# Gathered expert rows in four parts of 32 tokens: products of one table beside sums of the other

## The chip, the cores and the metric

The kernel runs on one core of one Trainium2 chip. The metric is the device time of one execution in microseconds. Three runs of the kernel before gave 3989.97, 3996.61 and 4001.97 us; the median is 3996.61.

## The reference, cut to what matters

Two layers, each a token mixer and then a product-key expert mixer ("peer"), over 512 tokens of width 1024. Only the expert mixer is touched. Each token picks 128 experts (8 heads, 16 each) out of 16384, and needs one row of table `u` and one of table `v` for each:

```python
def peer(h, w_q, sub_keys, u_emb, v_emb):
    q = (t @ w_q).reshape(n_tok, PEER_HEADS, 2, PEER_KEY_DIM // 2)
    scores = jnp.einsum('thpk,hpnk->thpn', q, sub_keys)
    ...
    best, pos = lax.top_k(cand, PEER_TOPK)
    expert = jnp.take_along_axis(cand_idx, pos, axis=-1)
    gates = jax.nn.softmax(best, axis=-1)
    ...
        u = u_emb[eb]
        act = jax.nn.gelu(jnp.einsum('td,thkd->thk', tb, u)) * gb
        return jnp.einsum('thk,thkd->td', act, v_emb[eb])
```

## The kernel before

The 512 tokens are four tiles of 128. Tiles 2 and 3 (`DT`) go the dense way: every row of both tables is read once, and a token's gate is zero for experts that it didn't pick. Tiles 0 and 1 (`GT`) go the gathered way: an indirect DMA fetches one table row for each of 128 partitions, so that 256 gathers a tile (128 of `u`, 128 of `v`) bring all it needs. Both ways run at the same time in one loop over 128 blocks of 128 experts.

The dense way, for block `b` (function `block`): `up` multiplies a block of `u` (24 bf16 matmuls `pu` of 256 columns: each fp32 operand is split in a high and a low bf16 half) and applies the gelu to give `H[b]`; DVE multiplies `H[b]` by the gate slice `G[:, j]` (tile `a`), ACT and DVE split it (`ah`, `al`), and twelve matmuls `acc` add `a` times the block of `v`. The weights come through `Stream.emit`: a 512 KB DMA, ACT makes `whi`, and GpSimd or, for 5 of 16 tiles, DVE makes `wlo`.

The gates are made in phases (`PHASES`): `gate_tile` holds the gates of 26 blocks (24 in the first phase) while those of the next phase are being made, in 16 groups of 16 tokens (`gate_group`). A group is an equality compare over all 128 keys (`o2`, 128x2048 elements), one over the phase's keys (`o1`), a multiply by the split gate, 16 small matmuls `pg`, two ACT copies `gs` and two adds into `G`. In the first phase the adds are GpSimd's; in all others everything but the copies is DVE's. The 16 groups of a phase are spread over the blocks of the phase before it; in the first phase they begin at block `LATE` = 13, when the routing of tile 1 is done, and must be done two blocks before the phase ends.

The gathered way (function `gathered`): a list `order` holds the gathers, first the 128 of `u` of tile 0, where partition t holds the row of token t, then the 128 of `v`, then the same for tile 1. A gather is queued on GpSimd (`gather`) right behind the newest weight split there, six places (`LEAD`) before its row is used; the rows lie in a ring of `ROWS` = 9 tiles. A `u` row is used by DVE: one `tensor_tensor_reduce` over 128x1024 (`products`, tile `junk`) gives 128 activations. Four `v` rows are used by PE (`sums`): eight fp32 matmuls, 32 columns of weights by 512, from which PE makes sixteen (`av`). The pace is set by `tick`, called once for each `up` and once for each block: it takes as many places of `order` as keep the list even over 222 ticks, a little over two each. Places taken before the loop (`EARLY_STEPS`) go beside the routing of tiles 2 and 3 and beside the first phase's 16 gate groups.

The order on each engine's queue is then set by a scheduler from the program's order and from explicit "issue after" constraints: products stand behind the newest split of `a`.

## Time and profile before

| | |
|---|---|
| Median of three runs | 3996.61 us |
| The profiled execution's own time | 3984.77 us |
| Its span, first to last instruction | 3982.9 us |
| PE, DVE, ACT, GpSimd busy | 79%, 73%, 37%, 66% of the span |
| Granted TensorE clock, mean | 0.883 |
| DMA | 923.70 MB, mean 232 GB/s |

The two layers stand one behind the other and read alike: in the first the expert mixer's early routing begins near 400 us, its gather queue at 501.8 us, its first gate phase at 640 us, and the loop over blocks runs from 729 to 1955 us; in the second the loop runs from 2739 to 3966 us. "Idle before" in a group's row is what its engine sat idle ahead of these instructions, and behind the arrows stands what ended it. DVE instructions overlap a little at their ends, so that the groups of a full stretch add up to some 6% more than the stretch.

### The profile page before, as it was taken

The numbers are of one execution on the slowest core, as the hardware profiler recorded it, in microseconds if no ns is written. First come the engines' busy times: TensorE is split into PE (matmuls) and PEld (weight loads), VectorE is DVE, ScalarE is ACT, GpSimd is POOL, SyncE is SP. The second block draws the span as 40 slices with busy tenths as digits, with TensorE's granted clock in tenths as the row PEclk, the third lists the DMA queues.
The fourth block names the chain that finished last, engine by engine and source line by source line (L and its number), as shares of the span: only waits on it lengthen the run. The fifth ranks groups of instructions, "written<-read, shape, count | busy, mean of one in ns | idle before, by whom it ended". The sixth has DMA issues, their size and how long they took to land. (4 is left out here: it accounts for less than half of the span.)

```text
span 3982.9 us, 53857 instructions
## 1 busy us (share of the span) xinstructions
PE 3138.0 (79%) x19594; PEld 1834.8 (46%) x19594; DVE 2911.0 (73%) x5135; ACT 1454.6 (37%) x2411; POOL 2638.5 (66%) x1721
## 2 busy tenths in 40 slices
PE   8999863567899766899898878635668997767998
PEld 4444552234455444454455545522344554444543
DVE  5553699998765999631568765999997559998524
ACT  5554432232333323332455564312323333333323
POOL 3446665665888878777433355657657888787875
PEclk9999986677999878999999999865778998888999
DMA  4324564576999888899621135654767999888997
GB/s 135 92 76 141 174 207 152 183 238 201 321 355 368 307 285 292 321 332 341 196 75 59 60 101 156 201 178 157 253 198 284 339 370 325 286 283 295 341 340 257
DMA packets 262346, 923.70 MB, mean 232 GB/s; under 512 B 29888, under 2 KB 39616, under 8 KB 262080
## 3 DMA queue, kind: packets, MB, share of 16 engines
q0 software_dynamic: 147456, 536.94, 37.8%
q1 hardware_dynamic: 104832, 372.84, 28.8%
q10 hardware_dynamic: 9792, 10.49, 0.9%
q8 instruction: 153, 2.51, 0.3%
q14 instruction: 113, 0.93, 0.1%
HBM read 918.05 MB, written 2.10 MB: 231 GB/s over the span
## 5 line engine op out<-in xcount | busy, mean ns | idle before, releaser
L81 POOL TENSOR_TENSOR wlo<-w,whi 128x1024 bf16<-128x1024 f32 x551 | 1220.9, 2220 | 596.9 <-ACT whi L80 554.3
L80 ACT ACTIVATE whi<-w 128x1024 bf16<-128x1024 f32 x696 | 731.5, 1053 | 829.3 <-DMA w<-ut_in 263.8
L764 POOL DMA_INDIRECT g<-u_in,ix x512 | 690.3, 1348 | 409.5 <-DVE hk L776 194.2
L776 DVE CUSTOM_DVE_ANT_0 junk<-g,hn 128x1024 bf16<-128x1024 f32 x512 | 754.7, 1474 | 6.1 <-DMA g<-u_in,ix 5.7
L764 POOL DMA_INDIRECT g<-v_in,ix x512 | 554.5, 1083 | 186.7 <-issue 94.3
L89 PE MATMUL pu<-hh,wlo 128*128 128x256 bf16 x2048 | 596.1, 291 | 72.6 <-DVE wlo L81 46.9
L87 PE MATMUL pu<-hh,whi 128*128 128x256 bf16 x2048 | 598.5, 292 | 29.5 <-ACT H L864 21.8
L88 PE MATMUL pu<-hl,whi 128*128 128x256 bf16 x2048 | 595.5, 291 | 0.0
L883 PE MATMUL pg<-o,o 128*128 128x52 bf16 (+1 forms) x2560 | 310.3, 282 | 355.0 <-DVE o L874 291.1
L81 DVE TENSOR_TENSOR al<-a,ah 128x256 bf16<-128x256 f32 x256 | 185.1, 723 | 510.9 <-ACT ah L80 507.5
L883 PEld LDWEIGHTS <-o 128*128 128x128 bf16 x2560 | 269.3, 149 | 431.0 <-DVE o L874 268.5
L88 PE MATMUL acc<-wlo,ah 128*128 128x512 bf16 x1024 | 433.3, 423 | 30.7 <-DVE wlo L81 29.4
L87 PE MATMUL acc<-whi,ah 128*128 128x512 bf16 x1024 | 376.0, 415 | 95.1 <-ACT ah L80 94.9
L89 PE MATMUL acc<-whi,al 128*128 128x512 bf16 x1024 | 422.8, 421 | 22.2 <-DVE al L81 22.0
L89 PEld LDWEIGHTS <-wlo 128*128 128x128 bf16 x2816 | 289.6, 103 | 202.4 <-DVE wlo L81 51.1
L799 PE MATMUL av<-g,z 128*32 128x512 f32 x2048 | 355.3, 605 | 17.5 <-DVE z L793 10.7
L87 PEld LDWEIGHTS <-whi 128*128 128x128 bf16 x2816 | 291.6, 104 | 153.9 <-issue 31.8
L88 PEld LDWEIGHTS <-whi 128*128 128x128 bf16 x2816 | 291.4, 103 | 138.6 <-issue 40.6
L885 ACT ACTIVATE gs<-pg 128x416 f32<-128x416 f32 (+1 forms) x320 | 163.3, 510 | 437.2 <-PE pg L883 427.1
L887 DVE TENSOR_TENSOR G<-gs 128x208 f32<-128x208 f32 x256 | 219.5, 860 | 86.2 <-ACT gs L885 85.9
L80 ACT ACTIVATE ah<-a 128x256 bf16<-128x256 f32 x256 | 105.8, 414 | 432.0 <-PE acc L88 196.1
L870 DVE TENSOR_TENSOR o<-iot,i2T 128x2048 bf16<-128x2048 bf16 x160 | 250.9, 1568 | 11.6 <-PE pg L883 11.2
(382 smaller groups left out, 5025.3 us busy)
## 6 DMA issues: line engine op xcount, KB each, us to landing
w<-ut_in SPq DMA_DIRECT2D x256, 512.0 KB, 5.3
w<-v_in SPq DMA_DIRECT2D x256, 512.0 KB, 5.0
w<-w_in SPq DMA_DIRECT2D x88, 512.0 KB, 3.6
w<-wo_in SPq DMA_DIRECT2D x64, 512.0 KB, 3.7
w<-wq_in SPq DMA_DIRECT2D x32, 512.0 KB, 3.6
key<-keys_in ACTq DMA_DIRECT2D x64, 128.0 KB, 3.2
g<-u_in,ix POOLq DMA_INDIRECT x512, 6.0
g<-v_in,ix POOLq DMA_INDIRECT x512, 7.0
```

What stands on the lines that cost most here:

```text
L80: nc.scalar.activation(hi, src, AF.Copy)
L81: return (lo_eng or nc.vector).tensor_tensor(lo, src, hi, op=OP.subtract)
L87: nc.tensor.matmul(out, ah, bh, start=start and i == 0, stop=False)
L88: nc.tensor.matmul(out, ah, bl, start=False, stop=False)
L89: nc.tensor.matmul(out, al, bh, start=False, stop=stop and i == n - 1)
L764: nc.gpsimd.indirect_dma_start(out=g, out_offset=None, in_=tab, in_offset=bass.IndirectOffsetOnAxis(ap=ix, axis=0))
L776: nc.vector.tensor_tensor_reduce(k.junk, g, hn[i], op0=OP.mult, op1=OP.add, scale=1.0, scalar=0.0, accum_out=h[:, s:s + 1])
L799: nc.tensor.matmul(av[c][32 * j:32 * j + 32, :], z[:, j, o:o + 32], rows[j][:, c * 512:(c + 1) * 512], start=r == 0, stop=r == 31)
L870: nc.vector.tensor_tensor(o2, iot, i2T[:, None, ts].to_broadcast([128, KEYS, GB]), op=OP.is_equal)
L883: nc.tensor.matmul(pv[:, t, :, :n], o2[:, :, c * 8 + t], o1[:, 1:3, :, c * 8 + t], start=True, stop=True)
L885: nc.scalar.activation(gs, pv[:, :, :, :n], AF.Copy)
L887: eng.tensor_tensor(G[:, :n, t0 + c * 8:t0 + c * 8 + 8], gv[:, 0], gv[:, 1], op=OP.add)
```

## The change

Three things change together.

1. The gathered tokens of a tile are taken in four parts (`PARTS`) of 32. In a gather of `u` the 128 partitions now hold 32 tokens times 4 experts each, so that 32 gathers serve a part; the part's own 32 rows of the normed input are copied four times over by matmuls with columns of the identity (`hr`). The list `order` now takes, in turns, four `u` gathers of part n and four `v` gathers of part n-1. The indices and gates of a tile are laid out for this at the end of its routing, by 32 small matmuls.
2. The eight `av` matmuls of four `v` rows are ordered behind the first of them, which waits for the row that comes last. The sums' two PSUM banks are held from the beginning, and `pg` in the first phase has 2 of them where it had 3.
3. `PHASES` is 18 and five times 22, six phases where there were five; `AHEAD` (the blocks whose `H` is made ahead) is 10 where it was 12, and the ring `ROWS` is 11 where it was 9. The compares at the end of the routing go in six pieces where they went in three.

```diff
-PHASES = [24, 26, 26, 26, 26]
+PHASES = [18, 22, 22, 22, 22, 22]
-AHEAD = 12
+AHEAD = 10
-ROWS = 9
+ROWS = 11
+PARTS = 4
...
+        def part(r):
+            return k.ident.rearrange("p (u r) -> p r u", r=PARTS)[:, r]
...
-            for j0, h0, nh in ((0, 0, 8), (8, 0, 4), (8, 4, 4)):
+            for j0, h0, nh in ((0, 0, 4), (0, 4, 4), (8, 0, 2), (8, 2, 2), (8, 4, 2), (8, 6, 2)):
...
-            def products(i, h):
-                for s in range(NS):
+            def products(i, r, h):
+                hr = work.tile([128, D], F32, tag="hr", name="hr", bufs=1)
+                for c in range(2):
+                    p = pr.tile([128, 512], F32, tag="r", name="phr")
+                    for q in range(4):
+                        nc.tensor.matmul(p[32 * q:32 * q + 32, :], part(r), hn[i][:, c * 512:(c + 1) * 512],
+                                         start=True, stop=True)
+                    nc.scalar.activation(hr[:, c * 512:(c + 1) * 512], p, AF.Copy)
+                for s in range(32):
                     g = yield
                     with after():
-                        nc.vector.tensor_tensor_reduce(k.junk, g, hn[i], op0=OP.mult, op1=OP.add, scale=1.0,
+                        nc.vector.tensor_tensor_reduce(k.junk, g, hr, op0=OP.mult, op1=OP.add, scale=1.0,
                                                        scalar=0.0, accum_out=h[:, s:s + 1])
-            def sums(i, h):
+            def sums(i, r, h, av):
...
+                    first = None
                     for c in range(2):
-                        for j in range(4):
-                            nc.tensor.matmul(av[c][32 * j:32 * j + 32, :], z[:, j, o:o + 32],
-                                             rows[j][:, c * 512:(c + 1) * 512], start=r == 0, stop=r == 31)
+                        for j in reversed(range(4)):
+                            with tc.issue_after(first.ins) if first is not None else nullcontext():
+                                m = nc.tensor.matmul(av[c][32 * j:32 * j + 32, :], z[:, j, a * 32:a * 32 + 32],
+                                                     rows[j][:, c * 512:(c + 1) * 512],
+                                                     start=r == 0 and a == 0, stop=r == PARTS - 1 and a == 7)
+                            first = first or m
...
-                for i in GT:
-                    order += [(ut, i, 0, s) for s in range(NS)]
-                    order += [(vt, i, 1, 32 * j + r) for r in range(32) for j in range(4)]
+                for n in range(len(parts) + 1):
+                    for a in range(8):
+                        if n < len(parts):
+                            order += [(n, 0, 4 * a + s) for s in range(4)]
+                        if n:
+                            order += [(n - 1, 1, 4 * a + j) for j in range(4)]
...
-                        pv = ahead.tile([128, 512], F32, tag="g", name="pg", bufs=3)
+                        pv = ahead.tile([128, 512], F32, tag="g", name="pg", bufs=2)
```

How the queues read. First GpSimd in the middle of layer 0's loop, where the gathers (`g`) and the weight splits (`wlo`) alternate. Before, in tile 0's sums:

```order
L764 DMA g<-v_in,ix_4182 128x1024 x4
L81 TENSOR_TENSOR wlo<-w_10389,whi 128x1024
L764 DMA g<-v_in,ix_4182 128x1024 x2
L81 TENSOR_TENSOR wlo<-w_10432,whi 128x1024
L764 DMA g<-v_in,ix_4182 128x1024 x2
L81 TENSOR_TENSOR wlo<-w_10492,whi 128x1024
```

After, at about the same place:

```order
L776 DMA g<-u_in,ix_4197 128x1024 x4
L82 TENSOR_TENSOR wlo<-w_9571,whi 128x1024
L776 DMA g<-v_in,ix_4197 128x1024 x2
L82 TENSOR_TENSOR wlo<-w_9622,whi 128x1024
L776 DMA g<-v_in,ix_4197 128x1024 x2
L776 DMA g<-u_in,ix_4197 128x1024 x2
```

The number of gathers between two splits is about the same; one table in long stretches has become both in turns of four.

Second, DVE in layer 0 at block 14 (`a` and `al` belong to a block, `o` and `G` to a gate group of the next phase, `junk` and `hk` to a product). Before, from block 14's `a` to block 15's:

```order
L922 TENSOR_TENSOR a_7135<-H,G 128x256
L870 TENSOR_TENSOR o_7165<-iot,i2T 128x2048
L81 TENSOR_TENSOR al<-a_7135,ah 128x256
L776 ISA junk,hk_4339<-g,hn_2721 128x1024
L776 ISA hk_4339 128x1
L872 TENSOR_TENSOR o_7167<-iot,i1T 128x416
...
L922 TENSOR_TENSOR a_7262<-H,G 128x256
```

After, from block 14's `a` to block 15's:

```order
L948 TENSOR_TENSOR a_7540<-H,G 128x256
L82 TENSOR_TENSOR al<-a_7326,ah 128x256
L915 TENSOR_TENSOR G<-gs 128x22x8
L795 ISA junk,hk<-g,hr 128x1024
...
L902 TENSOR_TENSOR o_7474<-o_7474,ghl 128x704
L82 TENSOR_TENSOR al<-a_7540,ah 128x256
...
L948 TENSOR_TENSOR a_7775<-H,G 128x256
```

Before, 18 rows stand between the two, with 2 gate groups and 4 products. After, 67 rows stand there, with 12 of the phase's 16 groups and 4 products, and 54 of them lie between block 14's `a` and its own `al`.

Third, PE in the sums of tile 1 (`av`) beside a block's matmuls (`acc`). Before, in layer 0:

```order
L89 MATMUL pu<-hh,wlo 128x256
L799 MATMUL av<-g,z 32x512 x2
L88 LDWEIGHTS ah
L88 MATMUL acc_6057<-wlo,ah 128x512
...
L799 MATMUL av<-g,z 32x512 x4
L87 LDWEIGHTS ah
L87 MATMUL acc_6057<-whi,ah 128x512
L799 MATMUL av<-g,z 32x512 x2
```

After, in the steady part of layer 0:

```order
L818 MATMUL av<-g,z 32x512 x4
L89 LDWEIGHTS ah
L89 MATMUL acc_6196<-wlo,ah 128x512
...
L818 MATMUL av<-g,z 32x512 x4
L88 LDWEIGHTS ah
L88 MATMUL acc_6196<-whi,ah 128x512
```

Before, the eight of a set were broken into runs of one to nine in tile 1's sums; after, they stand in runs of eight, or of four and four, in both tiles.

## Rows read from the trace of the kernel before

**Rows 1.** The page's 40 slices: DVE's busy share in tenths
```profile
DVE  5553699998765999631568765999997559998524
```
**Rows 2.** Windows of layer 0: us, busy us (instructions) per engine, granted clock, DMA share, GB/s
```profile
640.00:729.00 89.00, 31.48 (x266) 26.85 (x267) 89.00 (x121) 17.90 (x39) 67.37 (x52) 0.50 0.39 122
729.00:838.00 109.00, 60.69 (x222) 24.95 (x222) 108.36 (x303) 26.57 (x38) 64.83 (x43) 0.74 0.67 221
838.00:914.00 76.00, 51.97 (x324) 34.78 (x322) 73.08 (x96) 22.09 (x35) 47.75 (x31) 0.76 0.73 239
914.00:1003.00 89.00, 63.39 (x347) 37.70 (x345) 78.05 (x116) 24.94 (x42) 47.18 (x33) 0.72 0.65 210
1003.00:1283.00 280.00, 257.82 (x1857) 148.77 (x1856) 181.09 (x204) 101.24 (x163) 235.37 (x171) 0.98 0.95 349
1286.00:1616.00 330.00, 231.84 (x1424) 149.66 (x1423) 322.92 (x420) 100.94 (x157) 265.32 (x170) 0.83 0.86 297
1616.00:1915.00 299.00, 287.67 (x1718) 139.55 (x1716) 107.94 (x141) 96.47 (x147) 229.10 (x174) 0.98 0.91 332
```
**Rows 3.** Window of layer 1 that answers to 1286 to 1616 us of layer 0
```profile
3299.00:3633.00 334.00, 239.03 (x1402) 151.77 (x1401) 325.64 (x421) 98.81 (x157) 273.69 (x170) 0.81 0.85 295
```
**Rows 4.** Gathers from 914 us on: count, ns minimum/median/maximum, first and last start
```profile
L764 POOL DMA_INDIRECT g<-v_in,ix x256: 933/951/1996, 1002.7 to 1914.8; - x128
L764 POOL DMA_INDIRECT g<-u_in,ix x153: 933/1175/1994, 913.8 to 1614.7; - x153
```
**Rows 5.** Groups, 1003 to 1283 us: count | busy us, mean ns | idle before, releasers
```profile
L764 POOL DMA_INDIRECT g<-v_in,ix x128 | 143.1, 1118 | 40.0 <-issue 23.3 <-PE av L799 8.7 <-PE pg L883 2.3
L81 POOL TENSOR_TENSOR wlo<-w,whi 128x1024 bf16<-128x1024 f32 x41 | 90.9, 2224 | 4.9 <-ACT whi L80 4.3
L799 PE MATMUL av<-g,z 128*32 128x512 f32 x480 | 64.6, 602 | 2.9 <-DMA g<-v_in,ix 2.8
...
L887 DVE TENSOR_TENSOR G<-gs 128x208 f32<-128x208 f32 x38 | 40.5, 1065 | 22.8 <-ACT gs L885 22.8
...
L81 DVE TENSOR_TENSOR al<-a,ah 128x256 bf16<-128x256 f32 x32 | 26.0, 814 | 61.3 <-ACT ah L80 61.1
```
**Rows 6.** Groups, 1286 to 1616 us
```profile
L776 DVE CUSTOM_DVE_ANT_0 junk<-g,hn 128x1024 bf16<-128x1024 f32 x121 | 180.0, 1488 | 1.9 <-DMA g<-u_in,ix 1.8
L764 POOL DMA_INDIRECT g<-u_in,ix x128 | 171.3, 1338 | 34.3 <-issue 25.2 <-PE av L799 2.3 <-DVE hk L776 2.1
L81 POOL TENSOR_TENSOR wlo<-w,whi 128x1024 bf16<-128x1024 f32 x41 | 94.5, 2304 | 30.2 <-ACT whi L80 29.7
...
L883 PE MATMUL pg<-o,o 128*128 128x52 bf16 x304 | 38.0, 284 | 77.7 <-DVE o L874 65.6 <-ACT gs L885 12.1
```
**Rows 7.** Groups, 1616 to 1915 us
```profile
L764 POOL DMA_INDIRECT g<-v_in,ix x128 | 134.0, 1047 | 49.8 <-issue 22.6 <-PE av L799 21.9 <-PE acc L89 1.5
L799 PE MATMUL av<-g,z 128*32 128x512 f32 x492 | 108.9, 600 | 4.3 <-DMA g<-v_in,ix 2.4 <-DVE z L793 1.8
L81 POOL TENSOR_TENSOR wlo<-w,whi 128x1024 bf16<-128x1024 f32 x42 | 91.9, 2187 | 20.4 <-ACT whi L80 19.8
```
**Rows 8.** Groups, 729 to 838 us
```profile
L776 DVE CUSTOM_DVE_ANT_0 junk<-g,hn 128x1024 bf16<-128x1024 f32 x31 | 37.7, 1217 | 0.0
```
**Rows 9.** Groups, 838 to 914 us
```profile
L870 DVE TENSOR_TENSOR o<-iot,i2T 128x2048 bf16<-128x2048 bf16 x8 | 14.1, 1763 | 0.0
...
L887 DVE TENSOR_TENSOR G<-gs 128x208 f32<-128x208 f32 x15 | 10.9, 730 | 2.9 <-ACT gs L885 2.9
...
L872 DVE TENSOR_TENSOR o<-iot,i1T 128x416 bf16<-128x416 bf16 x8 | 7.8, 975 | 0.0
...
L874 DVE TENSOR_TENSOR o<-o,ghl 128x832 bf16<-128x832 bf16 x8 | 4.7, 586 | 0.0
```
**Rows 10.** PE in order of time, 1100 to 1830 us: start, us, what
```profile
1108.25 1.92 PE L799 MATMUL av<-g,z 128*32 128x512 f32 x16
...
1817.70 1.90 PE L799 MATMUL av<-g,z 128*32 128x512 f32 x4
```

More of the change, by code (lines that the diff above doesn't have):

```diff
@@ L721, in routing @@
                 idx[i] = one.tile([128, 2, NS], I32, name=f"ix{i}")
-                nc.vector.tensor_copy(idx[i][:, 0], eff)
                 gates[i] = one.tile([128, NS], F32, name=f"gt{i}")
-                nc.vector.tensor_copy(gates[i], gtf)
-                pt = pr.tile([128, 4, 128], F32, tag="r", name="pt")
-                nc.tensor.transpose(pt[:, 0], eff, k.ident)
-                nc.vector.tensor_copy(idx[i][:, 1], pt[:, 0])
+                pt = pr.tile([128, 3, 128], F32, tag="r", name="pt")
+                nc.tensor.transpose(pt[:, 2], eff, k.ident)
+                for r in range(PARTS):
+                    for q in range(4):
+                        for m, src in enumerate((eff, gtf)):
+                            nc.tensor.matmul(pt[32 * q:32 * q + 32, m, r * 32:(r + 1) * 32], part(r),
+                                             src[:, 32 * q:32 * q + 32], start=True, stop=True)
+                nc.vector.tensor_copy(idx[i], pt[:, 0:3:2])
+                nc.scalar.activation(gates[i], pt[:, 1], AF.Copy)
                 return
@@ new lines, in sums @@
+                nc.vector.tensor_mul(h, h, gates[i][:, r * 32:(r + 1) * 32])
+                pt = pr.tile([128, 4, 8], F32, tag="r", name="pt")
+                for q in range(4):
+                    nc.tensor.matmul(pt[32 * q:32 * q + 32].rearrange("p a b -> p (a b)"), h,
+                                     k.ident[:, 32 * q:32 * q + 32], start=True, stop=True)
+                z = work.tile([128, 4, 8 * 36], F32, tag="z", name="z")
+                nc.gpsimd.memset(z, 0.0)
+                nc.vector.tensor_copy(z.rearrange("p j (a x) -> p j a x", x=36)[:, :, :, r], pt)
@@ L801, in sums @@
-                    rows.clear()
-                for c in range(2):
-                    xs = k.x[i][:, c * 512:(c + 1) * 512]
-                    nc.vector.tensor_add(xs, xs, av[c])
-            def wanted():
-                for i in GT:
-                    h = one.tile([128, NS], F32, name=f"hk{i}")
-                    yield products(i, h)
-                    yield sums(i, h)
+                        for j in reversed(range(4)):
[4 more added lines that the diff above has]
+                            first = first or m
@@ new lines, in gathered @@
+                rows, users, h, av = [], {}, {}, {}
+                for m in range(len(order) + LEAD):
+                    if m < len(order):
+                        n, v, s = order[m]
+                        i, r = parts[n]
+                        at = 32 * (s % 4) + 4 * (s // 4) + r if v else 32 * r + s
+                        rows.append(gather((ut, vt)[v], idx[i][:, v, at:at + 1]))
+                    if m >= LEAD:
+                        n, v, s = order[m - LEAD]
+                        i, r = parts[n]
+                        if s == 0:
+                            if v == 0:
+                                h[n] = work.tile([128, 32], F32, tag="hk", name="hk")
+                                users[n, 0] = products(i, r, h[n])
+                            else:
+                                if r == 0:
+                                    av[i] = [accv.tile([128, 512], F32, tag=f"av{c}", name="av") for c in range(2)]
+                                users[n, 1] = sums(i, r, h[n], av[i])
+                            next(users[n, v])
@@ L830, in gathered @@
                         try:
[L831 removed]
+                            users[n, v].send(rows.pop(0))
                         except StopIteration:
[L833 removed]
+                            pass
                     yield
```

39 lines of the change are left out of this document (10 added, 29 removed).

## The prediction, made before the changed kernel was run

> **What bounds the kernel now.** I read the page's 40 slices first. DVE's row [rows 1] has the same figure twice, once a layer: a run of 9s, a valley of 6s, again 9s, then down to 2. So the loop's bound changes over time, and totals say little. Cutting layer 0 into windows [rows 2] gives the stages. From 640 to 914 us DVE is full (89.0 of 89, 108.4 of 109, 73.1 of 76); PE has 0.50 to 0.76 of its clock. From 1003 to 1283, tile 0's `v` rows, DVE is busy 181 of 280 us, PE 258, the DMA engines 0.95. From 1286 to 1616, tile 1's `u` rows, DVE is busy 323 of 330 and PE 232 at 0.83 of the clock. From 1616 to 1915, tile 1's `v` rows, PE is busy 288 of 299 and DVE 108. Layer 1 repeats it: its `u` window takes 334 us with DVE 326 [rows 3]. So I work out one layer and double it.
>
> The natural unit is the gather, since the pace list spreads them evenly over the loop. 128 gathers stand in each of the three long windows [rows 5 to 7]: 280/128 = 2.19 us a gather with `v` of tile 0, 330/128 = 2.58 with `u` of tile 1, 299/128 = 2.34 with `v` of tile 1. Together 912/384 = 2.37.
>
> Last I looked at GpSimd, because it issues every gather and makes 11 of 16 `wlo`. Its gathers, their idle before them and its splits make (143.1 + 40.0 + 90.9)/128 = 2.14 us a gather in the first window [rows 5], (171.3 + 34.3 + 94.5)/128 = 2.34 in the second [rows 6], (134.0 + 49.8 + 91.9)/128 = 2.15 in the third [rows 7]. It is not the busiest engine anywhere, but taking those idle gaps as part of its work it stands at 98%, 91% and 92% of the pace. That decides my forecast: DVE and PE can be averaged against each other; GpSimd and the DMA engines serve both kinds of row alike and cannot.
>
> **The change, step by step, for one layer.** Counts are from the order of instructions; durations from the rows.
>
> Up to block 0: the first gate phase makes 18 keys for 24. Scaled from the groups of 26 keys [rows 9], o1 (0.975) and the gate product (0.587) lose 6/26 of 1.56 = 0.36 us, 16 times = 6 us; 40 products stand ahead of block 0 instead of 42, 2 us. DVE is full there [rows 2]: -8 us. The adds into `G` are GpSimd's in that phase and shrink too, hidden behind DVE. The split compares of the routing, nine more instructions a tile with the same elements, and 32 tiny matmuls for the layout: under 1 us each by the smallest DVE rows, taken as nothing; if not, +5.
>
> Blocks 0 to 11: 20 products instead of 31, at 1.217 us [rows 8], DVE full: -13 us. PE gets sums there, but is busy only 61 of 109 us at 0.74 of the clock.
>
> Blocks 12 to 15: the 16 groups of phase 1 now go here; before, only 8 did. A group costs (14.1 + 7.8 + 4.7 + 10.9)/8 = 4.7 us [rows 9]; with 22 keys the last three shrink by 22/26, 4.2 us. 16 x 4.2 - 8 x 4.7 = +30. Products fall from 22 to 4: 18 x 1.22 = -22. Sum +8, DVE the bound in both. Behind the waiting `al` of block 14 stand that block's `acc` on PE, then the weight buffers, then the splits on GpSimd; they wait 45 us or so (10 of the groups), and the 10 blocks that `H` reaches ahead don't help. It costs no more than DVE's own time, which is counted.
>
> So block 16 begins at 914 - 13 = 901 us, with one place more taken from the list than before, and all of phase 1's gates made.
>
> From block 16 to the last gather: before, 409 gathers from 914 to 1915 us [rows 4], 1001 us. After, 407. What each engine needs for one gather, in an even mix:
> - DVE: 322.9/128 = 2.52 in the `u` window, of which products 180.0/128 = 1.41 [rows 2, 6]. Half the products, 0.70, plus 1.12 for the rest. Gates come 16 per 22 blocks instead of 26, 18% more groups at 0.9 of the price, +0.05 on the 0.70 that 19 groups cost. 1.87.
> - PE: 257.8/128 = 2.01 in the `v` window, less half its `av` (64.6/128/2 = 0.25), plus 18% of `pg` (38.0/128 = 0.30) = 0.05, plus the copies of 32 rows, as many matmuls of the same shape as a set of `av`, 1.92 us [rows 10] per 64 gathers, 0.03. 1.84; at the `u` window's clock (0.83 for 0.98) 2.17.
> - The DMA engines: 0.95 x 280, 0.86 x 330 and 0.91 x 299 us [rows 2] over 128: 2.08, 2.22, 2.13; mean 2.14. No byte is saved.
> - GpSimd: the mean of the `u` and the `v` window, (2.14 + 2.34)/2 = 2.24. A gather's mean is 1.338 us beside products and 1.118 without [rows 5, 6], and DVE at 1.87 of a pace near 2.3 lies between those windows, so the mean is the row nearest.
>
> GpSimd's 2.24 is the largest. The pace before lay 0.05 above its need in the first window, 0.23 in the second, where DVE was full, and 0.18 in the third, where PE was. I add the mean of the two windows in which DVE has air, 0.12: 2.36 us. 407 x 2.36 = 960 us, -41.
>
> The tail behind the last gather, 40 us, stays: block count and list end together in both.
>
> Also in this: the sets of `av` no longer break up. Sixteen instructions back to back take 1.92 us, four alone 1.90 [rows 10], and the third window pays 108.9 us for what the first does in 64.6 [rows 5, 7]. That 44 us is gain only where PE binds, and my PE need above uses the unbroken price; it isn't counted twice. Eleven row tiles for nine loosen the ring. At nothing I cost the start of a part: `hr` has one buffer, so a part's first product waits for PE and ACT behind the last product of the part before. Four `v` gathers lie between, 9 us, cover enough; uncovered it is some 4 us (1.92 and two ACT copies), eight times a layer, 32 us.
>
> Sum for a layer: -8 - 13 + 8 - 41 = -54; for two, -108. From the profiled execution's own 3984.8 us that is 3877. The three runs' median lies 12 us above that execution, so I state 3889.
>
> **The rivals.**
>
> Faster still: the gathers no longer wait on DVE, and the DMA engines set the pace at what the first window shows, 2.19 us. For it: in that window three engines ran above 90% together. Against: gathers beside products take 0.22 us longer. 407 x 2.19 = 891, -110; with -13 that is -123 a layer, 3751 on the median's scale. The Trainium skill's "SBUF — State Buffer", section "Who interferes with whom", speaks for this: a DVE instruction with two SBUF inputs contends with GpSimd only when that one reads SBUF, and it infers that making descriptors writes. By that rule all gathers would sit near the 933 ns minimum. The trace differs: beside products the median is 1175 against 951 [rows 4].
>
> No change, or nearly: with DVE busier on average, every gather pays the `u` window's price, 1.338 us. Need 2.34, pace 2.46, 1001 us: the loop gains nothing and only the -13 stays, 3971. The same section says that whoever is second waits until the first has finished, whole; the maxima near 2 us on either table [rows 4] agree, and half the gathers now change sides from a less busy DVE to a busier one.
>
> Slower: DVE's queue, in order, becomes the bound through waits rather than work. In the first window DVE sat idle 61.3 us for `ah` and 22.8 for `gs` [rows 5], 0.66 us a gather; in the `u` window it had neither, because products were always ready. If products now also wait for rows and these waits come back whole, a gather takes 1.87 + 0.66 = 2.53, 407 x 2.53 = 1030, +29 - 13 = +16 a layer: 4029. It turns to a loss from a pace of (1001 + 13)/407 = 2.49, that is when 0.62 of the 0.66 stays. Against it: DVE has products of several rows queued, and the ring is longer. The 32 us of `hr`, if uncovered, would push the same way.
>
> **How the numbers follow.** Forecast 0.60; still faster 0.10; nearly no change 0.14, half of it within 0.3%; slower 0.16. About 0.3% (12 us) is what a measurement of this kernel can tell from no change. Faster by more: 0.60 + 0.10 + 0.07 less 0.02 for the forecast's own edge, 0.75; within 0.09; slower 0.16. The forecast's own range goes from a pace without slack, 2.24 (912 us, -102 a layer, 3793), to 2.45 (997, -17, 3963). For 8 in 10 I reach halfway into the fast rival, 3765, and past the no-change case, 4010.
>
> **What would show it.** Right: no window of the loop with DVE above 97% but the burst near block 14; DVE and PE both near 80% and GpSimd with its gaps near 95% all along; gathers of both tables near 1.23 us; a granted clock near 0.9 throughout; some 2.36 us a gather. Wrong: DVE idle before `al`, `G` and `junk` at a pace above 2.49 (the slow rival); gathers at 1.34 (no change); or GpSimd idle for rows to be freed. If blocks 12 to 16 take more than 90 us, the burst costs more than DVE's work.

## The result, and the profile after

The kernel after takes 3878.73 us, median of four runs (3868.11 to 3885.22), against 3994.85 us for four runs of the kernel before beside it: ratio 0.9705, 95% interval 0.9677 to 0.9734. Forecast was 3889 us, with a range from 3793 to 3963, and faster.

The profiled execution took 3882.88 us; its span is 3881.1 us and its mean granted clock 0.893, where before had 0.883. Two rows of the page's 40 slices of the kernel after:

```profile
DVE  6553688899998988975568864889989878889863
...
DMA  4224565576899999999621125555758998999997
```

The valley in the middle of each layer's loop [rows 1] is gone: in the first layer DVE stays at 8 or 9 from the first gates to the 17th slice, and the DMA engines at 8 or 9 from the 11th slice on. Then, when the last gates are made (1734 us) and the last products done (1800 us), DVE falls to 7 and 5. Windows of layer 0, columns as in [rows 2]; the first three end at about block 0, block 12 and block 16, the last three hold 128, 130 and 128 gathers:

```profile
640.00:747.00 107.00, 38.18 (x330) 23.75 (x330) 98.40 (x240) 17.85 (x43) 69.97 (x62) 0.53 0.53 160
747.00:840.00 93.00, 64.81 (x314) 29.64 (x319) 91.42 (x281) 26.95 (x40) 65.09 (x45) 0.83 0.74 262
840.00:920.00 80.00, 59.53 (x478) 40.49 (x482) 68.09 (x103) 25.60 (x49) 35.45 (x23) 0.69 0.48 168
977.00:1282.00 305.00, 259.67 (x1795) 158.58 (x1823) 271.89 (x346) 109.03 (x181) 261.14 (x171) 0.93 0.92 326
1282.00:1584.00 302.00, 251.79 (x1730) 149.61 (x1759) 263.19 (x328) 106.29 (x173) 258.76 (x174) 0.91 0.93 330
1584.00:1866.00 282.00, 238.17 (x1598) 137.15 (x1625) 197.06 (x241) 99.20 (x154) 246.59 (x172) 0.91 0.96 349
```

The stage with DVE full and the one with PE full have become stretches that look alike. PE and DVE are each busy 83% to 89% of the first two long windows, at a clock of 0.91 to 0.93; 0.83 and 0.98 stood side by side before [rows 2]. In the third window, where gates and products end, DVE is busy 70% and the DMA engines 0.96. The groups from 977 to 1282 us, columns as in [rows 5]:

```profile
L795 DVE CUSTOM_DVE_ANT_0 junk<-g,hr 128x1024 bf16<-128x1024 f32 x66 | 114.9, 1740 | 14.9 <-DMA g<-u_in,ix 10.4 <-ACT whi L81 3.8
L82 POOL TENSOR_TENSOR wlo<-w,whi 128x1024 bf16<-128x1024 f32 x42 | 97.4, 2318 | 11.6 <-ACT whi L81 10.7 <-issue 0.2
L776 POOL DMA_INDIRECT g<-v_in,ix x64 | 85.5, 1336 | 15.7 <-issue 9.8 <-DVE a L948 1.2 <-DVE o L898 0.9
L776 POOL DMA_INDIRECT g<-u_in,ix x64 | 77.7, 1214 | 16.7 <-issue 13.2 <-DMA w<-v_in 0.6 <-PE pu L90 0.5
...
L915 DVE TENSOR_TENSOR G<-gs 128x176 f32<-128x176 f32 x49 | 43.6, 895 | 5.5 <-ACT gs L913 5.3
...
L818 PE MATMUL av<-g,z 128*32 128x512 f32 x256 | 36.2, 641 | 5.2 <-DMA g<-v_in,ix 3.2 <-DVE z L808 2.1
...
L82 DVE TENSOR_TENSOR al<-a,ah 128x256 bf16<-128x256 f32 x32 | 21.7, 678 | 8.1 <-ACT ah L81 8.1
...
L789 PE MATMUL phr<-hn,ident 128*32 128x512 f32 x32 | 7.6, 619 | 5.2 <-ACT hr L791 3.3 <-ACT gs L913 1.9
```

GpSimd's gathers, the idle before them and its splits make (85.5 + 77.7 + 15.7 + 16.7 + 97.4)/128 = 2.29 us a gather; the window's pace is 305/128 = 2.38. DVE's idle before `al` and `G`, 61.3 and 22.8 us before [rows 5], is 8.1 and 5.5. The groups of GpSimd in the next two windows:

```profile
L82 POOL TENSOR_TENSOR wlo<-w,whi 128x1024 bf16<-128x1024 f32 x42 | 96.4, 2296 | 10.3 <-ACT whi L81 9.6
L776 POOL DMA_INDIRECT g<-u_in,ix x65 | 82.1, 1264 | 16.4 <-issue 12.1 <-PE acc L90 1.8 <-DVE a L948 0.9
L776 POOL DMA_INDIRECT g<-v_in,ix x65 | 80.0, 1230 | 16.7 <-issue 11.8 <-DVE o L902 1.5 <-DMA w<-ut_in 0.6
...
L776 POOL DMA_INDIRECT g<-v_in,ix x80 | 95.6, 1194 | 20.7 <-issue 18.5 <-DVE o L902 0.3 <-PE acc L90 0.3
L82 POOL TENSOR_TENSOR wlo<-w,whi 128x1024 bf16<-128x1024 f32 x42 | 93.7, 2231 | 2.9 <-ACT whi L81 2.2
...
L776 POOL DMA_INDIRECT g<-u_in,ix x48 | 56.0, 1167 | 12.1 <-issue 9.1 <-PE pu L90 0.9 <-PE av L818 0.3
```

They need 2.24 at a pace of 2.32, and 2.17 at 2.20. Over the three windows: need 2.235, pace 2.303. What the need leaves out is, by the way it is added up, little more than GpSimd's idle before `wlo` (11.6, 10.3 and 2.9 us); so a pace close above the need says that GpSimd hardly stands still but for the gaps of some 0.25 us around each gather. Both tables' gathers now cost alike, which answers to [rows 4] (all gathers of layer 0 from 914 us on):

```profile
L776 POOL DMA_INDIRECT g<-v_in,ix x220: 933/1079/1997, 931.4 to 1865.6; - x110
...
L776 POOL DMA_INDIRECT g<-u_in,ix x185: 933/1092/2010, 929.3 to 1790.7; - x185
```

Where the time went, in us from each layer's first gather (layer 0 / layer 1; the start of a block is that of its `a` on DVE; each figure is rounded by itself):

| | before | after | change | forecast |
|---|---|---|---|---|
| start to block 0 | 228 / 228 | 242 / 239 | +14 / +11 | -8 |
| blocks 0 to 11 | 109 / 100 | 94 / 99 | -15 / -1 | -13 |
| blocks 12 to 15 | 76 / 78 | 80 / 71 | +4 / -7 | +8 |
| block 16 to the last gather | 1001 / 1011 | 945 / 953 | -55 / -58 | -41 |
| last gather to block 127 | 39 / 39 | 35 / 39 | -4 / 0 | 0 |
| sum | 1452 / 1455 | 1396 / 1400 | -56 / -55 | -54 |

The sum is right to 2 us a layer, but the steps are not: the start is some 20 us worse and the long stretch some 15 us better than forecast. Outside the table 3 us more pass before layer 0's first gather (504.7 for 501.8 us) and 6 more between layer 0's last block and layer 1's first gather. So the profiled execution gained 102 us (3984.77 to 3882.88) where the forecast for it was 108.

### The profile page after: what moved, and what is told of

The parts are those of the page before. It is cut to its first block, busy times and chain, and to the rows that moved or that the text cites. A ratio compares the mean times of both kernels' runs of the same rounds, so it can differ in the third digit from the quotient of the medians.

```text
span 3881.1 us, 55985 instructions
## 1 busy us (share of the span) xinstructions
PE 3079.0 (79%) x20451; PEld 1841.6 (47%) x20742; DVE 3022.6 (78%) x5371; ACT 1484.7 (38%) x2519; POOL 2654.7 (68%) x1721
## 5 line engine op out<-in xcount | busy, mean ns | idle before, releaser
L795 DVE CUSTOM_DVE_ANT_0 junk<-g,hr 128x1024 bf16<-128x1024 f32 x512 | 808.0, 1578 | 94.3 <-DMA g<-u_in,ix 83.8
L776 POOL DMA_INDIRECT g<-u_in,ix x512 | 618.3, 1208 | 255.1 <-issue 99.4
L776 POOL DMA_INDIRECT g<-v_in,ix x512 | 637.2, 1245 | 143.1 <-issue 98.3
L911 PE MATMUL pg<-o,o 128*128 128x44 bf16 (+1 forms) x3072 | 327.9, 266 | 312.0 <-DVE o L902 176.7
L90 PE MATMUL acc<-whi,al 128*128 128x512 bf16 x892 | 355.5, 403 | 21.5 <-DVE al L82 20.3
L88 PE MATMUL acc<-whi,ah 128*128 128x512 bf16 x953 | 311.5, 396 | 32.7 <-ACT ah L81 18.8
L818 PE MATMUL av<-g,z 128*32 128x512 f32 x2048 | 291.1, 675 | 54.2 <-DMA g<-v_in,ix 47.1
L913 ACT ACTIVATE gs<-pg 128x352 f32<-128x352 f32 (+1 forms) x384 | 174.0, 454 | 403.4 <-PE pg L911 281.0
L915 DVE TENSOR_TENSOR G<-gs 128x176 f32<-128x176 f32 x320 | 246.9, 779 | 59.4 <-ACT gs L913 49.8
L892 ACT ACTIVATE H<-pu 128x256 f32<-128x256 f32 x232 | 87.8, 378 | 385.5 <-PE pu L90 330.0
```

The costliest lines, as they stand in the source:

```text
L88: nc.tensor.matmul(out, ah, bh, start=start and i == 0, stop=False)
L90: nc.tensor.matmul(out, al, bh, start=False, stop=stop and i == n - 1)
L776: nc.gpsimd.indirect_dma_start(out=g, out_offset=None, in_=tab, in_offset=bass.IndirectOffsetOnAxis(ap=ix, axis=0))
L795: nc.vector.tensor_tensor_reduce(k.junk, g, hr, op0=OP.mult, op1=OP.add, scale=1.0, scalar=0.0, accum_out=h[:, s:s + 1])
L818: m = nc.tensor.matmul(av[c][32 * j:32 * j + 32, :], z[:, j, a * 32:a * 32 + 32], rows[j][:, c * 512:(c + 1) * 512], start=r == 0 and a == ...
L911: nc.tensor.matmul(pv[:, t, :, :n], o2[:, :, c * 8 + t], o1[:, 1:3, :, c * 8 + t], start=True, stop=True)
```

## The experiments

The theory to be tested: GpSimd's queue (gathers, the gaps around them, splits) sets the pace of the loop after the change, and the turns of four `u` and four `v` brought the gain by making DVE and PE even. The rivals: DVE sets it; PE and the clock set it; the DMA engines set it; or other parts of the change (the order of `av`, the ring, the phases) brought the gain.

### Who sets the pace: the share of splits

`SHARE` is how many of 16 `wlo` splits are DVE's and not GpSimd's. It moves work between the two engines and touches no byte and no matmul.

```diff
-SHARE = 5
+SHARE = 2
```

> The changed kernel with 2 of 16 weight splits on DVE instead of 5, so that GpSimd makes 3 of 16 more, 11 or so in 128 gathers at 2.3 us: +0.2 us of GpSimd a gather, and 0.12 us less of DVE. If GpSimd sets the pace in the steady loop: 0.2 x 407 gathers x 2 layers = 150 us or somewhat less, 3960 to 4040. If DVE's queue sets it: no longer, or 30 to 80 us shorter. If the DMA engines set it: within 30 us.

Measured: 3994.85 us, ratio to before 0.998 (0.9965 to 0.9996); against the kernel after 116 us slower, which loses the whole gain. A window of 128 gathers of this kernel, then its groups on GpSimd:

```profile
1308.00:1624.00 316.00, 259.70 (x1752) 154.27 (x1779) 269.61 (x316) 106.23 (x174) 277.68 (x184) 0.90 0.89 314
```
```profile
L82 POOL TENSOR_TENSOR wlo<-w,whi 128x1024 bf16<-128x1024 f32 x54 | 122.6, 2271 | 7.7 <-ACT whi L81 6.8
...
L776 POOL DMA_INDIRECT g<-v_in,ix x64 | 78.5, 1227 | 15.6 <-issue 10.3 <-DVE o L902 0.9 <-DMA w<-ut_in 0.9
L776 POOL DMA_INDIRECT g<-u_in,ix x64 | 75.0, 1172 | 15.2 <-issue 12.6 <-PE acc L90 0.8 <-DVE al L82 0.3
```

Twelve more splits a window raise the need to 2.40 us and the pace to 316/128 = 2.47. DVE (85%), PE (82%) and the DMA engines (0.89) all went down in share: none of them is nearer to full in this kernel, and the pace is slower all the same.

```diff
-SHARE = 5
+SHARE = 7
```

> The changed kernel with 7 of 16 weight splits on DVE instead of 5: in 128 gathers some 7 to 8 splits of 2.3 us leave GpSimd, 0.13 us a gather, and come to DVE at 1.4 us, 0.09 a gather. GpSimd theory: its need falls from 2.27 to 2.14 us a gather, the DMA engines' 0.92 to 0.96 share is met next at about 2.15 to 2.2; pace 2.20 to 2.28 instead of 2.32, 30 to 90 us shorter. DVE theory: DVE, at 2.04 to 2.12 of 2.36 us, goes to 2.15 to 2.2 and the kernel is 20 us or more longer. DMA theory: within 15 us.

Measured: 3801.61 us, 0.9518 (0.9472 to 0.9563), 77 us faster than the kernel after. The same two views of this kernel, 126 gathers:

```profile
1260.00:1543.00 283.00, 242.41 (x1685) 146.79 (x1712) 246.63 (x325) 103.95 (x168) 242.16 (x161) 0.92 0.93 341
```
```profile
L795 DVE CUSTOM_DVE_ANT_0 junk<-g,hr 128x1024 bf16<-128x1024 f32 x62 | 94.6, 1526 | 4.4 <-DMA g<-u_in,ix 3.1 <-ACT hr L791 0.6
L776 POOL DMA_INDIRECT g<-u_in,ix x64 | 83.7, 1308 | 16.2 <-issue 12.4 <-PE pu L90 0.9 <-PE pg L911 0.3
L776 POOL DMA_INDIRECT g<-v_in,ix x62 | 81.3, 1311 | 16.9 <-issue 12.4 <-DVE al L82 0.9 <-PE acc L89 0.3
L82 POOL TENSOR_TENSOR wlo<-w,whi 128x1024 bf16<-128x1024 f32 x33 | 75.0, 2273 | 7.8 <-ACT whi L81 7.3
```

Need (83.7 + 81.3 + 16.2 + 16.9 + 75.0)/126 = 2.17, pace 2.25. Take these two windows and the second long one of the kernel after: over 2.17, 2.24 and 2.40 us of need the pace is 2.25, 2.32 and 2.47. From block 16 to the last gather, 405 gathers in each of the three kernels, layer 0 takes 909, 945 and 1005 us and layer 1 takes 921, 953 and 1008.

That the pace lies 0.07 to 0.08 above the need each time proves little, since this remainder is mostly GpSimd's idle before `wlo`, left out of the need. The evidence is that the time follows both signs, while bytes and matmuls stay the same and DVE, busy 85 to 87% of these windows, stands idle in all three. A gain alone could have come from elsewhere. The gaps belong to the need, too, as far as they stay what they are, 0.24 to 0.26 us a gather in all three windows and mostly ended by "issue". The need moved by less than the splits that were moved: twelve splits of 2.27 us are 0.21 us a gather, but it rose by 0.16, since the gathers with their gaps cost 1.57, 1.50 and 1.44 us at seven, five and two splits on DVE. One rival is left. DVE's own time falls as it takes splits on, 2.11, 2.02 and 1.96 us a gather at two, five and seven, since its products become shorter (mean 1526 ns at seven, 1740 in the first long window of the kernel after). So a part of the gain may come by way of DVE; these runs do not separate the two.

### What the turns brought

The kernel after with all 128 `u` of a tile first and then its 128 `v`, everything else as it is (with eight `hk` buffers, since the activations of four parts now wait):

```diff
-                for n in range(len(parts) + 1):
-                    for a in range(8):
-                        if n < len(parts):
-                            order += [(n, 0, 4 * a + s) for s in range(4)]
-                        if n:
-                            order += [(n - 1, 1, 4 * a + j) for j in range(4)]
+                for n in range(0, len(parts), PARTS):
+                    for v in range(2):
+                        order += [(n + r, v, s) for r in range(PARTS) for s in range(32)]
```

> The changed kernel with its turns undone alone: parts, layout, phases, rings and unbroken sets stay, but all 128 gathers of u of a tile come first and then its 128 of v. Turns theory: almost the whole gain is lost, the windows part again into DVE-full (2.5 to 2.6 us a gather) and PE-full ones; 3960 to 4020 us. Set theory, or one in which rings or phases bring the gain: within 30 us of the changed kernel's 3879.

Measured: 3938.92 us, 0.9849 (0.983 to 0.9868). So the turns are worth 60 us, about half of the 116, and the range that I gave the turns began above this time. The windows of this kernel with tile 0's `v` rows, tile 1's `u` rows and tile 1's `v` rows:

```profile
1003.00:1292.00 289.00, 266.44 (x1996) 159.30 (x2027) 210.89 (x242) 107.89 (x176) 237.70 (x173) 0.97 0.93 344
1292.00:1621.00 329.00, 236.03 (x1493) 145.62 (x1516) 312.94 (x416) 105.93 (x174) 260.75 (x172) 0.85 0.85 302
1621.00:1895.00 274.00, 255.07 (x1847) 144.41 (x1880) 141.77 (x186) 102.13 (x161) 230.51 (x173) 0.95 0.96 360
```

DVE and PE trade places again, as in [rows 2], and the clock with them. But the three windows take 892 us for 384 gathers, 2.32 us each, hardly more than the 2.30 of the mixed kernel: what the `u` rows lose (2.57) the `v` rows win back (2.26 and 2.14). The 60 us lie elsewhere. This is what taking one part out of the kernel after costs at each step, by the traces (layer 0 / layer 1, in us; the last two columns belong to the runs further down):

| | without turns | without the order of `av` | nine row tiles |
|---|---|---|---|
| start to block 0 | -3 / +2 | 0 / +3 | -2 / +7 |
| blocks 0 to 11 | +20 / +13 | -4 / -2 | +1 / -2 |
| blocks 12 to 15 | +3 / +12 | -2 / +2 | -6 / +4 |
| block 16 to the last gather | +9 / +5 | +24 / +29 | +15 / +10 |
| last gather to block 127 | 0 / -2 | +1 / +2 | -1 / -1 |

Most of what the turns bring, 23 and 25 us a layer, lies in the first 16 blocks. There DVE is full or nearly so (113.3 of 113.6 us in blocks 0 to 11 without turns), and the turns put 24 products of 1.2 us where 48 stand without them. In the long stretch, where averaging DVE and PE was to pay, undoing the turns costs only 9 and 5 us, though it also leaves 32 fewer products there (160 for 192), and how much that hides is not settled. Counted from the first gather, the kernel without turns reaches block 40 behind the kernel after by 27 and 29 us, block 84, where its second `u` rows end, by 60 and 66, and block 127 by 29 and 31: what it loses later in `u` rows it wins back in `v` rows.

A coarser turn, 32 `u` of one part, then 32 `v` of the part before (and four `hk` buffers):

```diff
-                    for a in range(8):
-                        if n < len(parts):
-                            order += [(n, 0, 4 * a + s) for s in range(4)]
-                        if n:
-                            order += [(n - 1, 1, 4 * a + j) for j in range(4)]
+                    if n < len(parts):
+                        order += [(n, 0, s) for s in range(32)]
+                    if n:
+                        order += [(n - 1, 1, s) for s in range(32)]
```

> The changed kernel with turns of 32 gathers instead of four: all 32 of u of a part, then all 32 of v of the part before. The averages over a part are the same, but 32 u gathers last some 75 us, longer than H is ahead or the ring holds. If only the averages count: within 15 us of 3879. If the buffers can't bridge a turn, the windows part again: 3920 to 3950, near the 3939 of the kernel without turns.

Measured: 3895.98 us, 0.9754 (0.9736 to 0.9772), 17 us above the kernel after. Two stretches of this kernel in a row:

```profile
1090.00:1165.00 75.00, 60.03 (x382) 36.02 (x381) 73.32 (x98) 24.88 (x40) 67.36 (x38) 0.87 0.87 300
1165.00:1240.00 75.00, 70.58 (x518) 42.05 (x517) 51.72 (x59) 27.71 (x45) 66.19 (x47) 0.98 0.96 353
```

The windows do part again: DVE is busy 98% in one and 69% in the next, PE 80% and 94%. I had expected 3920 us at least in that case. The kernel reaches block 62 level with the kernel after (4 us behind and 0) and loses 13 and 6 us by block 127. So windows with DVE nearly full beside windows with PE nearly full cost little as such.

### The other parts, each alone

The kernel before, with the eight `av` of a set ordered behind the first (the edit in the change's `sums`, and nothing else of it):

```diff
+                    first = None
                     for c in range(2):
-                        for j in range(4):
-                            nc.tensor.matmul(av[c][32 * j:32 * j + 32, :], z[:, j, o:o + 32],
-                                             rows[j][:, c * 512:(c + 1) * 512], start=r == 0, stop=r == 31)
+                        for j in reversed(range(4)):
+                            with tc.issue_after(first.ins) if first is not None else nullcontext():
+                                m = nc.tensor.matmul(av[c][32 * j:32 * j + 32, :], z[:, j, o:o + 32],
+                                                     rows[j][:, c * 512:(c + 1) * 512], start=r == 0, stop=r == 31)
+                            first = first or m
```

> The kernel before with one part of the change: the eight av matmuls of a set stand behind the first, which waits for the last row. Turns theory (the gain comes from taking both tables in turns, and GpSimd's gathers and splits then set the pace): only the third long window of each layer, 299 and 292 us, where PE is full, can gain, at most 44 us of PE a layer; its pace falls from 2.34 to the first window's 2.19, 19 us a layer, so 20 to 40 us off in all. Set theory (the gain of 116 us is mostly that PE no longer pays for broken sets): 80 us off or more.

Measured: 3963.53 us, 0.992 (0.9891 to 0.9948), some 32 us, within what the turns theory expected. From 1635 to 1911 us this kernel is in tile 1's `v` rows, as the kernel before in [rows 7]:

```profile
L764 POOL DMA_INDIRECT g<-v_in,ix x127 | 134.2, 1056 | 42.6 <-issue 26.9 <-PE av L801 13.0 <-PE acc L88 0.9
L81 POOL TENSOR_TENSOR wlo<-w,whi 128x1024 bf16<-128x1024 f32 x42 | 90.5, 2155 | 4.6 <-ACT whi L80 3.0 <-issue 0.8
...
L801 PE MATMUL av<-g,z 128*32 128x512 f32 x488 | 63.2, 631 | 20.3 <-DMA g<-v_in,ix 19.5 <-issue 0.6
```

`av` costs 63.2 us for 488 instructions, where 492 cost 108.9 [rows 7]. GpSimd's need is (134.2 + 42.6 + 90.5)/127 = 2.10, the pace 276/127 = 2.17; before, 2.15 and 2.34. So of the 0.17 us that the pace fell, 0.05 is need and the rest was GpSimd's idle before `wlo`. That PE was behind this idle is argued from the edit, which touches PE alone. In the profiled execution the earlier windows of layer 0 give most of it back: its three long windows take 298, 337 and 276 us, where the kernel before has 283, 330 and 299.

The reverse, the kernel after without that order:

```diff
-                        for j in reversed(range(4)):
-                            with tc.issue_after(first.ins) if first is not None else nullcontext():
+                        for j in range(4):
+                            with nullcontext():
```

> The changed kernel with the order of the eight av matmuls given up, so that the sets break into runs of one to nine again. PE has 15 to 20% air at this pace; broken sets cost it up to 44 us a layer for 128 gathers of v, 0.17 us a gather in the mix. GpSimd theory: hidden for the most part, 0 to 30 us longer. If PE's stalls in order count as in the kernel before: 30 to 70 us longer.

Measured: 3944.44 us, 0.9881 (0.9864 to 0.9897), 65 us above the kernel after; the theory of GpSimd as the only bound expected 30 at most. A window of 129 gathers of this kernel, and GpSimd's splits and `av` in it:

```profile
974.00:1291.00 317.00, 290.25 (x1821) 160.94 (x1822) 266.91 (x348) 109.03 (x180) 265.01 (x173) 0.96 0.89 314
```
```profile
L82 POOL TENSOR_TENSOR wlo<-w,whi 128x1024 bf16<-128x1024 f32 x43 | 100.5, 2338 | 19.3 <-ACT whi L81 18.6
...
L818 PE MATMUL av<-g,z 128*32 128x512 f32 x256 | 71.6, 613 | 4.5 <-DMA g<-v_in,ix 2.9 <-DVE z L808 1.6
```

`av` doubles, 71.6 us for 36.2, PE is busy 92% of 317 us, and the pace is 2.46 for 2.38 in the kernel after; in the next window it is 303/129 = 2.35. GpSimd's idle before `wlo` in the first window is 19.3 us for 11.6. So PE is a second bound, close behind GpSimd: of 0.28 us a gather more on PE, 0.08 came through to the pace. Under turns the order is worth twice what it is worth alone (65 against 32 us), and nearly all of it lies in the long stretch.

The kernel before with the phases alone:

```diff
-PHASES = [24, 26, 26, 26, 26]
+PHASES = [18, 22, 22, 22, 22, 22]
...
-AHEAD = 12
+AHEAD = 10
```

> The kernel before with six gate phases (18 and five of 22) and 10 blocks of H ahead, gathers and rings as before. Turns theory: the phases are a price, one more set of 16 groups a layer at 4.2 us on DVE in stretches that are partly full, and the first groups crowded into three blocks: 10 to 50 us longer in all. A theory in which the smaller gate tiles bring the gain: 50 us shorter or more.

Measured: 4007.18 us, 1.0017 (1.0001 to 1.0032): 7 us lost, a little less than I expected. Block 0 comes 10 and 6 us earlier (218 and 221 us after the first gather), which is the -8 that I forecast for this step; blocks 12 to 15, with 96 us in either layer for 76 and 78, give it back.

The kernel after with the ring of before:

```diff
-ROWS = 11
+ROWS = 9
```

> The changed kernel with the ring of rows back at 9 tiles. With all undone but turns and unbroken sets this shows what the two extra tiles give. Ring theory (the 60 us that the kernel without turns still gained, less 32 for unbroken sets and plus 7 for the phases, came from the ring): 30 to 60 us longer than the changed kernel. Otherwise, rows are freed in time anyway: within 15 us.

Measured: 3902.77 us, 0.9761 (0.9741 to 0.9781), 24 us lost, between the two expectations. By the table above the loss lies in the long stretch. I had put no number on the ring.

### Why block 0 is late, and the burst at block 14

With nine row tiles there is room for the compares in three pieces, as the kernel before had them (`eq` and `em` become twice as large for it):

```diff
-            for j0, h0, nh in ((0, 0, 4), (0, 4, 4), (8, 0, 2), (8, 2, 2), (8, 4, 2), (8, 6, 2)):
+            for j0, h0, nh in ((0, 0, 8), (8, 0, 4), (8, 4, 4)):
```

> The changed kernel with the ring at 9 tiles (that makes the room) and the routing's compares in three pieces as before, to be held against the one with 9 tiles and six pieces. By the profile the compares of two tiles cost DVE 46 us in six pieces and 35 in three ahead of block 0, where DVE binds: 10 to 25 us shorter in all (four gate-way and gathered tiles, two layers), block 0 some 10 us earlier behind the first gather. If the pieces don't matter, block 0 stays where it is and the time within 8 us.

Measured: 3895.86 us, 0.9758 (0.9728 to 0.9787). The kernel with nine row tiles alone takes 7 us more, and the two intervals overlap, so as a time this is unclear. As a place it is clear: block 0 stands at 224 and 229 us instead of 240 and 246. By the end little of these 16 us is left, since the pace list only spreads the gathers over what follows.

The kernel after with the first gate groups from block 10:

```diff
-LATE = 13
+LATE = 10
...
-                        for _ in itertools.islice(others, 3):
+                        for _ in itertools.islice(others, 4):
```

> The changed kernel with the first groups of the next phase from block 10 instead of 13 (tile 1's routing in four pieces a block instead of three, done by block 10): 16 groups over six blocks instead of three. If the burst only costs DVE's own work, as forecast: within 15 us. If it starves PE, GpSimd and the weight ring for some 50 us a layer that the steady loop could have used: 20 to 80 us shorter.

Measured: 3874.54 us, 0.9699 (0.9676 to 0.9723), the same as the kernel after. Spreading the 16 gate groups over more blocks gains nothing measurable, as it should be if the burst costs only DVE's own work.

### Was GpSimd a bound before, too?

The kernel before, with the share alone:

```diff
-SHARE = 5
+SHARE = 7
```

> The kernel before with 7 of 16 weight splits on DVE instead of 5. Turns theory: the move pays only where DVE has air all along. In the windows with u rows DVE is full (323 of 330 us, twice a layer in part) and takes 7 to 8 more splits of 1.57 us, 12 us longer a window; in the first window with v rows GpSimd gains 0.13 us a gather, 17 us, if PE lets it; in the third PE is full. Sum within 30 us of 3997 either way. If moving splits pays anywhere alike, as in the changed kernel: 60 us shorter or more.

Measured: 3900.75 us, 0.9774 (0.9751 to 0.9796), 90 us faster. My expectation fell, but not for the reason that the rival gives. The three long windows of layer 0, 128 gathers each, then the gathers of the first window, and the gathers, splits and `av` of the third (one gather starts outside it):

```profile
995.00:1277.00 282.00, 260.20 (x1862) 151.40 (x1862) 177.59 (x212) 100.51 (x161) 220.40 (x165) 0.96 0.94 346
1277.00:1599.00 322.00, 235.52 (x1418) 147.64 (x1418) 305.19 (x412) 99.86 (x157) 251.51 (x163) 0.84 0.89 311
1599.00:1864.00 265.00, 251.73 (x1735) 137.24 (x1733) 139.93 (x165) 97.52 (x151) 218.06 (x164) 0.99 0.97 367
```
```profile
L764 POOL DMA_INDIRECT g<-v_in,ix x128 | 143.9, 1124 | 51.7 <-issue 23.1 <-PE av L799 15.4 <-DVE hk L776 5.6
```
```profile
L764 POOL DMA_INDIRECT g<-v_in,ix x127 | 142.2, 1119 | 43.9 <-issue 24.1 <-PE av L799 9.8 <-DVE hk L776 5.1
L81 POOL TENSOR_TENSOR wlo<-w,whi 128x1024 bf16<-128x1024 f32 x34 | 73.6, 2167 | 4.9 <-ACT whi L80 4.3
L799 PE MATMUL av<-g,z 128*32 128x512 f32 x480 | 71.6, 599 | 3.3 <-DMA g<-v_in,ix 3.2
```

The first window takes what it took before, 282 us for 283 from the first of these gathers to the next tile's: seven splits left GpSimd, but its gathers waited longer (51.7 us for 40.0 [rows 5], of which 15.4 for `av`, where it was 8.7). The second wins 8 us, although DVE is nearly full there and took splits on. The third wins most, 265 us for 299: the need fell from 2.15 to (142.2 + 43.9 + 73.6)/127 = 2.04, the pace from 2.34 to 2.09, more than that. There `av` costs 71.6 us instead of 108.9, which came unasked, with another order of the queues. So that GpSimd bound the kernel before is not shown by this run, and how much of the 90 us is the splits and how much the sets of `av` stays open.

### A version that beats both

```diff
-LATE = 13
+LATE = 10
...
-SHARE = 5
+SHARE = 8
...
-                        for _ in itertools.islice(others, 3):
+                        for _ in itertools.islice(others, 4):
```

> The changed kernel with 8 of 16 splits on DVE and the first groups from block 10. GpSimd theory: need 2.15 - 0.06 = 2.09 us a gather, DMA engines near 0.97: pace 2.15 to 2.22, 3740 to 3800. If the DMA engines or DVE (near 90% with 7 of 16) have taken over already: 3790 to 3830.

Measured: 3784.56 us, 0.9477 (0.9461 to 0.9493), the fastest here. The kernel with seven shares takes 17 us more, but the two intervals overlap (0.9472 to 0.9563 there) and `LATE` differs as well, so what the eighth share brings is not clear; it is less than the two before it brought, 77. A window of this kernel:

```profile
960.00:1250.00 290.00, 258.55 (x1813) 158.18 (x1814) 260.91 (x357) 109.34 (x181) 238.35 (x160) 0.92 0.93 345
```

PE and DVE stand at 89% and 90% and the DMA engines at 0.93, while GpSimd is at 82%, for 86% in the kernel after: little seems left in this lever.

## Why the prediction was right, and where it was not

**Right: the bound after the change, and its size.** "DVE and PE can be averaged against each other; GpSimd and the DMA engines serve both kinds of row alike and cannot." The forecast need of GpSimd was 2.24 us, measured 2.235, and a gather's mean was to be 1.23 us and is 1.235; of the DMA engines 2.14, measured (0.92 x 305 + 0.93 x 302 + 0.96 x 282)/386 = 2.16. The two runs on the share show that the time follows GpSimd's share of the splits in both directions. PE stands close behind, and the DMA engines at 0.92 to 0.96 are not far off.

**Wrong: where the turns pay.** The sum lays -41 us a layer, the whole gain of the long stretch, on the averaging of DVE and PE. Undoing the turns costs 9 and 5 us there; giving up the order of `av` costs 24 and 29, and nine row tiles cost 15 and 10. The order was in the text ("gain only where PE binds"), but not in the sum, and the ring had no number. The turns paid in the first 16 blocks instead, by 23 and 25 us, where the sum had 13 and 22 us for products that no longer stand there: that step was right in kind. Over all, undoing the turns costs 60 us of 116, undoing the order 65 (32 alone), two row tiles 24, the phases alone lose 7; these overlap and don't add up.

**Mis-sized: the slack.** I took 0.12 us, half-way between two windows before. The three windows after show 0.09, 0.08 and 0.03. But 0.12 also had to pay for the start of the stretch, where the 19 gathers from block 16 to 977 us take 3 us each. Over the stretch the pace is 945/405 = 2.33 us for the forecast 2.36, which is 10 us; 5 more are two gathers that were taken earlier. In layer 1 the stretch took 953 us for the forecast 960; the rest of the -58 is that before it had taken 1011 there, while I doubled layer 0. Of the third window's 0.18 before, the order of `av` alone took away 0.11: that part was the price of broken sets, and I had put it into one mean with its neighbour's 0.05.

**Failed: "Up to block 0 ... -8 us".** It came 14 and 11 us later, and 3 and 6 us were lost ahead of it. The smaller phase does give 10 and 6, as the run with the phases alone shows. The step that failed is "DVE is full there": it holds before and not after. From layer 0's first gather to block 0, before and after (the third figure with a count is DVE's):

```profile
501.80:729.30 227.50, 114.62 (x854) 91.22 (x852) 218.29 (x624) 60.44 (x109) 146.00 (x102) 0.70 0.55 173
```
```profile
504.70:746.60 241.90, 125.03 (x920) 88.48 (x918) 214.47 (x642) 60.74 (x114) 144.51 (x111) 0.70 0.58 184
```

DVE's work fell by 4 us, and in layer 1 by 10 (221.3 to 211.5), near the forecast; but its idle time rose from 9 to 27 us, and in layer 1 from 6 to 27. Two of the rows before which it stood, from the kernel before and then from the kernel after:

```profile
L870 DVE TENSOR_TENSOR o<-iot,i2T 128x2048 bf16<-128x2048 bf16 x16 | 28.7, 1791 | 0.0
...
L652 DVE MAX8 wk<-sc 128x8 f32<-128x128 f32 x36 | 10.0, 284 | 8.7 <-ACT sc L648 8.6
```
```profile
L898 DVE TENSOR_TENSOR o<-iot,i2T 128x2048 bf16<-128x2048 bf16 x16 | 23.0, 1436 | 7.1 <-PE pg L911 7.1
...
L657 DVE MAX8 wk<-sc 128x8 f32<-128x128 f32 x36 | 10.3, 292 | 17.0 <-ACT sc L653 12.2 <-issue 4.7
```

The compares of the routing, which I took "as nothing; if not, +5", cost 46.4 us in 36 instructions for 34.6 in 18; shorter gate groups and fewer products made up for that. With the split undone block 0 came 16 us earlier than with nine row tiles alone, part of it DVE's work (207.6 for 217.2 us in layer 0, 213.8 for 216.1 in layer 1), part idle time. The waits for `pg` are new, and `pg` has two banks there for three; no run gives the third bank back, so what it costs stays open.

Two errors of 15 to 22 us each, with opposite signs, made the total look better than its working. That the table's sum came out within 2 us a layer is luck.

**The signs that I named.** GpSimd with its gaps is at 97% of the pace, as said (95%), and the burst took 80 and 71 us, below the 90 that would have spoken against it. But DVE is above 97% in blocks 0 to 11, too (91.4 of 93 us), and the granted clock is 0.83 and 0.69 up to block 16, not near 0.9.

**The covers held.** Products wait 2.0 us for `hr` in the whole execution. The slow rival's wait (0.66 us a gather for `al` and `G`) shrank to 13.6 us in 128 gathers, 0.11.

**Too low: DVE and PE.** Forecast 1.87 and 1.84 us a gather, measured 2.12 and 2.03 in the first long window and 2.02 and 1.94 in the second. For PE the clock explains about half in the first and all in the second: 1.84 at 0.98 is 1.94 at 0.93 and 1.98 at 0.91. For DVE it is mostly the products, 114.9/128 = 0.90 us a gather for 0.70, since I halved their cost with their number. All products from 977 to 1282 us of the kernel after (minimum, median, maximum in ns):

```profile
L795 DVE CUSTOM_DVE_ANT_0 junk<-g,hr x66: 1205/1224/3735, 974.4 to 1281.3; 128x1024 bf16<-128x1024 f32 x66
```

The median is 1224 ns and the mean 1740. Of the 65 that start inside the window 47 take about 1.22 us, and each of the 18 others (mean 3.0 us) runs beside a `wlo` of GpSimd. In the next window it is 16 of 64. Before, in tile 1's `u` windows, it was 15 of 121 in layer 0 and 26 of 122 in layer 1. The number of collisions did not halve with the products.

## What to carry to other kernels

For each stage ask which engine serves all kinds of its work: what it needs for one unit, with the gaps around its own short instructions, is a pace that mixing can't beat, and moving work off it (here 2 of 16 splits, 77 us) may be worth as much as the reordering. That an engine is full before a change does not say that it will be full after it; ask what it will wait for. Test a bound with both signs, put each part of a combined change on the chip alone, and read its effect stage by stage: a right total can hide errors that cancel, and a part can pay in another stage than the one it was meant for.

## What was not expected of the hardware

A 128x1024 product on DVE mostly takes 1.22 us, and otherwise mostly 2.5 to 3.9 us. In the whole trace before 62 of 512 products are over 1.7 us, in the one after 99 of 512, and each of them runs beside a `wlo` of GpSimd, but for six of 1.7 to 1.9 us, which run beside one of GpSimd's adds into `G`. The reverse does not hold: 12 of the 47 short ones in the window from 977 us lie beside a `wlo`, too. The Trainium skill's "SBUF — State Buffer", section "Who interferes with whom", says that a DVE instruction with two SBUF inputs contends with a GpSimd instruction that reads SBUF; these long products agree with it, at some 1.8 us each in the window after and 2.2 in tile 1's `u` window before. The share of such meetings differs much between kernels: 10 of 61 with seven splits in 16 moved, 6 of 104 with long stretches of one table. Why, no run here settles.
